# Two k groups instead of one by seven products in each gate/up pair, with one weight sum made by an accumulating DMA

## The chip, the cores and the metric

The kernel runs on one core of one Trainium2 chip. The metric is device time in microseconds (us). Engines: PE (TensorE matmul), DVE (VectorE), ACT (ScalarE), POOL (GpSimd), SP (SyncE, which here only issues DMAs).

## The reference

A two-layer decoder over 256 tokens of width 2048, in float32: a Mamba-2 mixer, a SwiGLU FFN, forgetting attention on shared keys and values, and another SwiGLU FFN. The change touches the large projections, above all the FFN's first one:

```
def swiglu(h, w_gate_up, w_down):
    g, u = jnp.split(h @ w_gate_up, 2, axis=-1)
    return (jax.nn.silu(g) * u) @ w_down
```

`h` is 256 x 2048, gate and up are 5632 columns each, and `w_down` is 5632 x 2048. Two such FFNs are run, one in each layer.

## The kernel before

**Tiles.** A weight matrix comes in units of 512 k rows by 512 columns (1024 KB), each loaded by one DMA on SP's queue into one of three buffers (`wraw`, RAW = 3). A unit holds four k tiles of 128 rows. For near-float32 accuracy each weight tile is split into a high part (`whi`, rounded by ACT, L260) and a low part (`wlo`, the rest, by DVE, L266), and a matmul is done as three: x high by w high, x high by w low, x low by w high (L506 to L508). A plain unit is split in two pieces of two k tiles, and PE does 12 matmuls of 512 columns for each piece. `whi` and `wlo` have four buffers each (SPL = 4), so a split can run up to four pieces ahead of PE.

**Pairs and crossed groups.** Two neighbouring blocks of 512 columns (gate and up of one block in the FFN) make a pair. For some k groups, given in `crossed`, the pair is computed by a seven-product scheme of the Strassen-Winograd kind: the four quarters of the weights (two k halves by two column blocks: b11, b21 in the gate buffer; b12, b22 in the up buffer) and the four quarters of x (two token halves by two k halves) are combined by sums, and seven products of six matmuls each (`cross_step`, L425 to L427) take the place of eight. The products are called d, g, a, c, e, b, f, and ORDER (L206) is their order in time. Sums of x are made once per slot (`sums_of`, `add_sums`); sums of weights are made on DVE in place, in the raw buffers, in `split_cross` (`add`, L384): four of them per group before the change. The products a, c, d, e are kept in four PSUM banks (`mis`) until the pair's last crossed group is done, and are then put together on DVE (`parts`).

**Which groups.** A gate/up pair has four k groups (0 to 3) and before the change crosses group 2 alone, `(2,)`. There are 11 pairs in each of the two FFNs. The other crossed groups are those of the output projection of the Mamba mixer (4 and 6, in two pairs), of the attention (2, two pairs) and of the two down projections (3, 7 and 3, 6, 9, in two pairs each). That makes 22 + 4 + 2 + 4 + 6 = 38 groups.

**Order of the work.** `stream` writes every engine's instructions in order. Units of a pair go in this order: the left units up to a crossed group, then the right units up to it, then the group, and so on. Loads are issued three units ahead: when the last split that reads a unit has been written, the load of the unit three places later follows on SP (`load_to`), and it waits until that split has run. `split_to` writes splits four pieces ahead of PE's step. Other work (evacuation, transposes into the next stage's x, sums of x) is held in queues by `Flow`, which lets it in where its model of the engines' time says that it is ready; before the first product d of a pair, all that is urgent or next in line is written out (`finish_all(False)`, L413).

Of the kernel before, what the change touches and what calls it, by code (L numbers as in the profile page):

```python
# [12 lines left out]
ALU = mybir.AluOpType  # L13
# [16 lines left out]
NFB = DFF // NB  # L30
# [4 lines left out]
KT = 4  # L35

WOUT, DN0, DN1 = (4, 6), (3, 7), (3, 6, 9)

WARM = 9
RAW = 3  # L40
# [8 lines left out]
C_AN, C_F0, C_KV, C_BN, C_F1 = 0, 16, 32, 48, 64  # L49
# [130 lines left out]
class Unit:  # L180


    def __init__(self, blk, kg, src, width, pieces):
        self.blk, self.kg, self.src, self.width, self.pieces = blk, kg, src, width, pieces
        self.raw = None


class Block:
# [8 lines left out]
class Cross:  # L197
# [5 lines left out]

    ORDER = "dgacebf"  # L206

    def __init__(self, left, right, parts):
        self.left, self.right, self.parts, self.ps = left, right, parts, {}
# [10 lines left out]
def kernel(ctx: ExitStack, tc: tile.TileContext, xT_d, x_d, cols_d, rows_d, wdt_d, win_d,  # L220
# [99 lines left out]
    def pair(xs, sources, done, fills, crossed, parts):  # L320


        both = [Block(xs, d, f) for d, f in zip(done, fills)]
        x = Cross(*both, parts)
        order, rights = [], []
        for kg in range(len(xs)):
            us = [Unit(b, kg, src[kg].rearrange("p (k n) -> p k n", n=NB), NB, [[0, 1], [2, 3]])
                  for b, src in zip(both, sources)]
            if kg in crossed:
                order += rights  # L330
                rights = []
                order.append(Group(x, us, xs[kg], kg == crossed[0], kg == crossed[-1]))
            else:
                for b, u in zip(both, us):
                    b.units.append(u)
                order.append(us[0])
                rights.append(us[1])
        blocks.append(order + rights)
# [8 lines left out]
    def load(u, apart=False, before=None):  # L347
        n = sum(len(p) for p in u.pieces)
        u.raw = wraw.tile([P, n, u.width], F32, tag="wraw", name=nm("wraw"))
        for ks in u.pieces if apart else [range(n)]:  # L350
            if before is not None:
                before(ks)
            nc.sync.dma_start(out=u.raw[:, ks[0]:ks[-1] + 1, :], in_=u.src[:, ks[0]:ks[-1] + 1, :])

    def split_piece(u, ks):
        n = len(ks)
# [19 lines left out]

    def split_cross(x, name):

        (g, u) = (v.raw.rearrange("p (j i) n -> p i j n", i=2) for v in x.units)
        b11, b21, b12, b22 = g[:, 0], g[:, 1], u[:, 0], u[:, 1]  # L380

        def add(out, in0, in1):
            flow.work("V", 1.22, flow.at["E"])
            nc.vector.tensor_tensor(out=out, in0=in0, in1=in1, op=ALU.add)  # L384

        src = {"d": b21, "g": b11, "a": b21, "c": b22, "e": b21, "b": b22, "f": b12}[name]
        hi = wspl.tile([P, 2, NB], F32R, tag="whi", name=nm("whi"))
        lo = wspl.tile([P, 2, NB], F32R, tag="wlo", name=nm("wlo"))
        split_hi(hi, src)
        if name == "g":  # L390
            add(b22, b12, b22)
        if name == "c":
            add(b21, b12, b21)
        split_lo(hi, lo, src)
        ready = flow.work("V", 1.22, flow.work("A", 1.05, flow.at["E"]) + LAT)
        if name == "d":
            add(b21, b21, b22)
        if name == "c":
            add(b22, b11, b21)
        return hi, lo, ready  # L400

    def cross_step(group, name, parts):
# [20 lines left out]
        for p in range(2):  # L423
# [1 line left out]
            nc.tensor.matmul(ps, lhsT=xh, rhs=hi[:, p, :], start=group.first and p == 0 and name not in own, stop=False)  # L425
            nc.tensor.matmul(ps, lhsT=xh, rhs=lo[:, p, :], start=False, stop=False)  # L426
            nc.tensor.matmul(ps, lhsT=xl, rhs=hi[:, p, :], start=False, stop=group.last and p == 1 and name not in own)  # L427
        if group.last and name == "e":
            spawn(x.parts(x))
        flow.work("E", STEP)  # L430
        flow.pump()
# [1 line left out]
    def stream(pre_load, pre_split):  # L433
# [12 lines left out]
        def load_to(n):  # L446
            while loaded[0] < min(n, len(units)):
                i = loaded[0]
                if i in pre_load:
                    pre_load[i]()  # L450
                load(units[i], i < 2, load_x0 if i == 0 else None)
                loaded[0] += 1

        def split_to(n):
            for i in range(len(parts), min(n, len(pieces))):
                u, ks = pieces[i]
                if isinstance(u, Group):
                    parts[i] = split_cross(u, ks)
                    if ks in "ef":
                        load_to(units.index(u.units["ef".index(ks)]) + 1 + RAW)  # L460
                    continue
                if i in pre_split:
                    pre_split[i]()
                parts[i] = split_piece(u, ks)
                if ks is u.pieces[-1]:
                    load_to(units.index(u) + 1 + RAW)
# [205 lines left out]
    def ffn_up(xs, r, gu_d, summed):  # L672
# [37 lines left out]
        for nb in range(NFB):  # L710
            x = [None]

            def took(y, x=x):
                x[0] = y
                return parts(y)

            pair(xs, gu_d[2 * nb:2 * nb + 2], (lambda ps, x=x: gate(x[0], ps), lambda ps, x=x, nb=nb: up(x[0], ps, nb)),
                 (None, acts[nb]), (2,), took)
        return acts


# [306 lines left out]
    for g in range(G):  # L1028
        wide(xs1, win_d[12 + g], z_done(g))

    xs2, r2 = out_stage(ys, wout_d, C_F0, WOUT, summed=(2,))
    act0 = ffn_up(xs2, r2, gu0_d, DN0)


# [176 lines left out]
        else:  # L1211
            wide(xsq, wv_d[j], v_done(j), wcol=C_KV)

    xs4, r4 = out_stage(oT, wo_d, C_F1, (2,), summed=(2,))
    act1 = ffn_up(xs4, r4, gu1_d, DN1)
    out_v = out_d.rearrange("(t p) d -> p t d", p=P)

# [103 lines left out]
```

## Time and profile before

| | us |
|---|---|
| median of three runs | 2517.35 (2516.65 to 2519.01) |
| profiled execution, its own time | 2517.21 |
| its span (first to last instruction) | 2515.4 |
| PE busy in the span | 2502.9 |
| DVE busy | 1938.8 |
| ACT busy | 1370.1 |
| DMA queue of SP | 52.5% of 16 engines' span |

Busy time of PE counts overlapping pipelined matmuls as one stretch. A matmul's length in the trace (0.39 us) is longer than the distance from one start to the next; it is the distance that sets the pace. DVE's instructions overlap a little in the same way (a length of 1.22 us, starts 1.14 us apart).

### The profile page before, as it was taken

How to read it: one execution, taken by the hardware profiler on the slowest of the kernel's cores; microseconds unless marked ns; L12 is line 12 of the kernel's file. 1: busy time of each engine (PE TensorE's matmuls, PEld its weight loads, DVE VectorE, ACT ScalarE, POOL GpSimd, SP SyncE). 2: the span in 40 equal slices, each digit the busy share in tenths (PEclk: the TensorE clock that was granted, in tenths of full speed). 3: DMA queues.
4: the chain of work that ended last, by engine and by line, in shares of the span. 5: the costliest groups of instructions: out<-in, count | busy, mean ns of one | idle time of the engine just before them, and what ended most of it. 6: DMA issues, size and time to landing. Idle time of an engine off the chain costs nothing.

```text
span 2515.4 us, 30043 instructions
## 1 busy us (share of the span) xinstructions
PE 2502.9 (100%) x11542; PEld 2076.0 (83%) x11542; DVE 1938.8 (77%) x2499; ACT 1370.1 (54%) x1733; POOL 39.5 (2%) x52
## 2 busy tenths in 40 slices
PE   9999999999999999999999999999999999999999
PEld 7888888887878888888888888888878888888887
DVE  7777777778788878788767667678887878879767
ACT  6665566555555555455545555655555555555544
POOL 0000000000000000000000000000000000000000
PEclk9999999999999999999999999999999999999999
DMA  7655455445554646465565555444555564645564
GB/s 269 223 175 174 178 182 203 167 168 196 186 203 168 218 167 223 178 217 184 181 216 187 200 175 203 163 168 170 182 182 203 184 215 169 219 167 206 200 230 150
DMA packets 68319, 481.11 MB, mean 191 GB/s; under 512 B 7600, under 2 KB 8256, under 8 KB 10576
## 3 DMA queue, kind: packets, MB, share of 16 engines
q1 hardware_dynamic: 66672, 468.64, 52.5%
q0 software_dynamic: 1504, 10.57, 1.0%
q8 instruction: 90, 1.47, 0.2%
q14 instruction: 53, 0.43, 0.0%
HBM read 477.00 MB, written 2.18 MB: 190 GB/s over the span
## 4 chain that ended last, share of the span: by engine, by line
PE 96%; DVE 3%; DMA 1%; ACT 0%; issue 0%; SPq 0%; ACTq 0%; DVEq 0%
PE acc L506 26%; PE acc L507 26%; PE acc L508 26%; PE mis L426 2%; PE mis L427 2%; PE mis L425 2%; PE acc L425 2%; PE acc L427 2%; PE acc L426 2%; PE mis L539 1%; DVE wlo L266 1%; PE mis L967 1%; DVE wraw L384 1%; PE mis L837 0%; DMA xraw<-in_xT_dram 0%; PE mis L973 0%
## 5 line engine op out<-in xcount | busy, mean ns | idle before, releaser
L266 DVE TENSOR_TENSOR wlo<-wraw,whi 128x1024 fp32r<-128x1024 f32 (+1 forms) x899 | 1079.7, 1220 | 349.1 <-ACT whi L260 341.2
L260 ACT CAST whi<-wraw 128x1024 fp32r<-128x1024 f32 (+1 forms) x902 | 929.4, 1049 | 740.4 <-PE acc L508 544.5
L506 PE MATMUL acc<-whi,xT 128*128 128x512 f32 x2816 | 1107.2, 393 | 0.5 <-ACT whi L260 0.4
L507 PE MATMUL acc<-wlo,xT 128*128 128x512 f32 x2816 | 1097.4, 390 | 1.0 <-DVE wlo L266 0.7
L508 PE MATMUL acc<-whi,xT 128*128 128x512 f32 x2816 | 1097.5, 390 | 0.0
L508 PEld LDWEIGHTS acc<-whi,xT 128*128 128x128 f32 x2816 | 528.9, 188 | 110.8
L507 PEld LDWEIGHTS acc<-wlo,xT 128*128 128x128 f32 x2816 | 529.4, 188 | 109.9 <-DVE wlo L266 2.6
L506 PEld LDWEIGHTS acc<-whi,xT 128*128 128x128 f32 x2816 | 529.3, 188 | 109.1 <-issue 1.2
L268 DVE SCALAR_TENSOR_TENSOR wlo<-wraw,cols,whi 128x512 fp32r<-128x512 f32 x192 | 134.6, 748 | 70.8 <-ACT whi L262 70.3
L262 ACT ACTIVATE whi<-wraw,cols 128x512 fp32r<-128x512 f32 x192 | 127.5, 717 | 72.2 <-PE acc L508 67.1
L384 DVE TENSOR_TENSOR wraw<-wraw,wraw 128x1024 f32<-128x1024 f32 x76 | 93.0, 1224 | 3.3 <-DMA wraw<-in_wout_dram 1.0
L384 DVE TENSOR_TENSOR wraw<-wraw 128x1024 f32<-128x1024 f32 x76 | 93.1, 1225 | 2.6
L426 PE MATMUL mis<-wlo,xS 128*128 128x512 f32 x228 | 89.5, 393 | 4.2 <-DVE wlo L266 4.2
L427 PE MATMUL mis<-whi,xS 128*128 128x512 f32 x228 | 88.7, 389 | 0.0
L425 PE MATMUL mis<-whi,xS 128*128 128x512 f32 x228 | 88.7, 389 | 0.0
L266 DVE TENSOR_TENSOR xT<-mis,xT 128x512 fp32r<-128x512 f32 x52 | 33.5, 686 | 37.2 <-ACT xT L260 37.2
L260 ACT CAST xT<-mis 128x512 fp32r<-128x512 f32 x52 | 27.9, 590 | 53.4 <-PE mis L539 53.4
L425 PE MATMUL acc<-whi,xT 128*128 128x512 f32 x144 | 56.1, 389 | 0.0
L427 PE MATMUL acc<-whi,xT 128*128 128x512 f32 x144 | 56.0, 389 | 0.0
L426 PE MATMUL acc<-wlo,xT 128*128 128x512 f32 x144 | 56.0, 389 | 0.0
L426 PEld LDWEIGHTS mis<-wlo,xS 128*128 128x128 f32 x228 | 42.8, 188 | 15.9 <-DVE wlo L266 7.3
L526 POOL TENSOR_TENSOR rs<-ms,mhalf 128x4 f32<-128x4 f32 (+1 forms) x27 | 30.2, 1119 | 1494.8 <-DVE ms L524 1494.5
(241 smaller groups left out, 1890.7 us busy)
## 6 DMA issues: line engine op xcount, KB each, us to landing
wraw<-in_gu_dram SPq DMA_DIRECT2D x176, 1024.0 KB, 4.9
wraw<-in_dn_dram SPq DMA_DIRECT2D x88, 1024.0 KB, 4.9
wraw<-in_win_dram SPq DMA_DIRECT2D x78, 1024.0 KB, 4.9
wraw<-in_wout_dram SPq DMA_DIRECT2D x32, 1024.0 KB, 5.0
wraw<-in_wq_dram SPq DMA_DIRECT2D x16, 1024.0 KB, 5.0
wraw<-in_wk_dram SPq DMA_DIRECT2D x16, 1024.0 KB, 4.9
wraw<-in_wv_dram SPq DMA_DIRECT2D x16, 1024.0 KB, 4.9
wraw<-in_wo_dram SPq DMA_DIRECT2D x16, 1024.0 KB, 4.9
```

What stands on the lines that cost most here:

```text
L260: nc.scalar.copy(out=hi, in_=src)
L262: nc.scalar.activation(hi, src, AF.Copy, scale=scal)
L266: nc.vector.tensor_tensor(out=lo, in0=src, in1=hi.bitcast(F32), op=ALU.subtract)
L268: nc.vector.scalar_tensor_tensor(out=lo, in0=src, scalar=scal, in1=hi.bitcast(F32), op0=ALU.mult, op1=ALU.subtract)
L384: nc.vector.tensor_tensor(out=out, in0=in0, in1=in1, op=ALU.add)
L425: nc.tensor.matmul(ps, lhsT=xh, rhs=hi[:, p, :], start=group.first and p == 0 and name not in own, stop=False)
L426: nc.tensor.matmul(ps, lhsT=xh, rhs=lo[:, p, :], start=False, stop=False)
L427: nc.tensor.matmul(ps, lhsT=xl, rhs=hi[:, p, :], start=False, stop=group.last and p == 1 and name not in own)
L506: nc.tensor.matmul(b.ps[t], lhsT=xh, rhs=hi[:, j, :], start=k == 0, stop=False)
L507: nc.tensor.matmul(b.ps[t], lhsT=xh, rhs=lo[:, j, :], start=False, stop=False)
L508: nc.tensor.matmul(b.ps[t], lhsT=xl, rhs=hi[:, j, :], start=False, stop=k == nk - 1)
L526: nc.gpsimd.tensor_tensor(out=r, in0=ms, in1=mhalf[:, :width], op=ALU.pow)
```

## The change

`ORDER` becomes d, g, c, e, a, b, f, with another choice of weight sums. Of the four sums of weights per group, three stay on DVE (after the splits of d, c and e), and the one that adds b12 to b22 is made by a DMA: when the up unit has landed, POOL issues a second DMA that reads half of the same unit from HBM (512 KB, in rows of 2 KB) and adds it to the other half in the buffer (`accum_op`). That holds for all crossed groups, those in the projections too. All gate/up pairs but the last of each FFN cross groups 1 and 2, one straight behind the other, instead of 2 alone: 20 pairs gain a group, and there are 58 groups in all. For that, slot 1 of x gets its sums too (`summed=(1, 2)`).

```diff
--- before.py
+++ after.py
@@ -182,7 +182,7 @@
 
     def __init__(self, blk, kg, src, width, pieces):
         self.blk, self.kg, self.src, self.width, self.pieces = blk, kg, src, width, pieces
-        self.raw = None
+        self.raw, self.summed = None, False
 
 
 class Block:
@@ -203,7 +203,7 @@
 
 
 
-    ORDER = "dgacebf"
+    ORDER = "dgceabf"
 
     def __init__(self, left, right, parts):
         self.left, self.right, self.parts, self.ps = left, right, parts, {}
@@ -327,6 +327,7 @@
             us = [Unit(b, kg, src[kg].rearrange("p (k n) -> p k n", n=NB), NB, [[0, 1], [2, 3]])
                   for b, src in zip(both, sources)]
             if kg in crossed:
+                us[1].summed = True
                 order += rights
                 rights = []
                 order.append(Group(x, us, xs[kg], kg == crossed[0], kg == crossed[-1]))
@@ -351,6 +352,9 @@
             if before is not None:
                 before(ks)
             nc.sync.dma_start(out=u.raw[:, ks[0]:ks[-1] + 1, :], in_=u.src[:, ks[0]:ks[-1] + 1, :])
+        if u.summed:
+
+            nc.gpsimd.dma_start(out=u.raw[:, 1:KT:2, :], in_=u.src[:, 0:KT:2, :], accum_op=ALU.add)
 
     def split_piece(u, ks):
         n = len(ks)
@@ -376,27 +380,26 @@
 
     def split_cross(x, name):
 
+
         (g, u) = (v.raw.rearrange("p (j i) n -> p i j n", i=2) for v in x.units)
         b11, b21, b12, b22 = g[:, 0], g[:, 1], u[:, 0], u[:, 1]
 
-        def add(out, in0, in1):
+        def add(out, in0, in1, op=ALU.add):
             flow.work("V", 1.22, flow.at["E"])
-            nc.vector.tensor_tensor(out=out, in0=in0, in1=in1, op=ALU.add)
-
-        src = {"d": b21, "g": b11, "a": b21, "c": b22, "e": b21, "b": b22, "f": b12}[name]
+            nc.vector.tensor_tensor(out=out, in0=in0, in1=in1, op=op)
+
+        src = {"d": b21, "g": b11, "a": b22, "c": b22, "e": b21, "b": b21, "f": b12}[name]
         hi = wspl.tile([P, 2, NB], F32R, tag="whi", name=nm("whi"))
         lo = wspl.tile([P, 2, NB], F32R, tag="wlo", name=nm("wlo"))
         split_hi(hi, src)
-        if name == "g":
-            add(b22, b12, b22)
-        if name == "c":
-            add(b21, b12, b21)
         split_lo(hi, lo, src)
         ready = flow.work("V", 1.22, flow.work("A", 1.05, flow.at["E"]) + LAT)
         if name == "d":
             add(b21, b21, b22)
         if name == "c":
-            add(b22, b11, b21)
+            add(b22, b21, b12, ALU.subtract)
+        if name == "e":
+            add(b21, b11, b21)
         return hi, lo, ready
 
     def cross_step(group, name, parts):
@@ -425,7 +428,7 @@
             nc.tensor.matmul(ps, lhsT=xh, rhs=hi[:, p, :], start=group.first and p == 0 and name not in own, stop=False)
             nc.tensor.matmul(ps, lhsT=xh, rhs=lo[:, p, :], start=False, stop=False)
             nc.tensor.matmul(ps, lhsT=xl, rhs=hi[:, p, :], start=False, stop=group.last and p == 1 and name not in own)
-        if group.last and name == "e":
+        if group.last and name == "a":
             spawn(x.parts(x))
         flow.work("E", STEP)
         flow.pump()
@@ -456,8 +459,8 @@
                 u, ks = pieces[i]
                 if isinstance(u, Group):
                     parts[i] = split_cross(u, ks)
-                    if ks in "ef":
-                        load_to(units.index(u.units["ef".index(ks)]) + 1 + RAW)
+                    if ks in "bf":
+                        load_to(units.index(u.units["bf".index(ks)]) + 1 + RAW)
                     continue
                 if i in pre_split:
                     pre_split[i]()
@@ -715,7 +718,7 @@
                 return parts(y)
 
             pair(xs, gu_d[2 * nb:2 * nb + 2], (lambda ps, x=x: gate(x[0], ps), lambda ps, x=x, nb=nb: up(x[0], ps, nb)),
-                 (None, acts[nb]), (2,), took)
+                 (None, acts[nb]), (1, 2) if nb < NFB - 1 else (2,), took)
         return acts
 
 
@@ -1028,7 +1031,7 @@
     for g in range(G):
         wide(xs1, win_d[12 + g], z_done(g))
 
-    xs2, r2 = out_stage(ys, wout_d, C_F0, WOUT, summed=(2,))
+    xs2, r2 = out_stage(ys, wout_d, C_F0, WOUT, summed=(1, 2))
     act0 = ffn_up(xs2, r2, gu0_d, DN0)
 
 
@@ -1211,7 +1214,7 @@
         else:
             wide(xsq, wv_d[j], v_done(j), wcol=C_KV)
 
-    xs4, r4 = out_stage(oT, wo_d, C_F1, (2,), summed=(2,))
+    xs4, r4 = out_stage(oT, wo_d, C_F1, (2,), summed=(1, 2))
     act1 = ffn_up(xs4, r4, gu1_d, DN1)
     out_v = out_d.rearrange("(t p) d -> p t d", p=P)
```

How the instructions stand on DVE, in the crossed group of a gate/up pair in the first FFN, before the change (a line that writes `wlo` is the low part of one product's split, in the order d, g, a, c, e, b, f; `wraw_1293` is the gate buffer, `wraw_1300` the up buffer):

```order
L266 TENSOR_TENSOR wlo_1312_7670<-wraw_1293_7564,whi_1311_7669 128x1024
L384 TENSOR_TENSOR wraw_1293_7564<-wraw_1293_7564,wraw_1300_7604 128x2x512
L384 TENSOR_TENSOR wraw_1300_7604<-wraw_1300_7604 128x2x512
L266 TENSOR_TENSOR wlo_1314_7687<-wraw_1293_7564,whi_1313_7686 128x1024
L266 TENSOR_TENSOR wlo_1316_7704<-wraw_1293_7564,whi_1315_7703 128x1024
L384 TENSOR_TENSOR wraw_1293_7564<-wraw_1300_7604,wraw_1293_7564 128x2x512
L266 TENSOR_TENSOR wlo_1318_7720<-wraw_1300_7604,whi_1317_7719 128x1024
L384 TENSOR_TENSOR wraw_1300_7604<-wraw_1293_7564 128x2x512
L266 TENSOR_TENSOR wlo_1321_7733<-wraw_1293_7564,whi_1320_7732 128x1024
L266 TENSOR_TENSOR wlo_1324_7745<-wraw_1300_7604,whi_1323_7744 128x1024
L266 TENSOR_TENSOR wlo_1327_7756<-wraw_1300_7604,whi_1326_7755 128x1024
```

Four sums (L384) stand among seven splits.

The same place in the changed kernel, from the last two splits of group 1 (b and f) through the whole of group 2 (`wraw_1267` its gate buffer, `wraw_1288` its up buffer):

```order
L266 TENSOR_TENSOR wlo_1287_7424<-wraw_1257_7241,whi_1286_7423 128x1024
L266 TENSOR_TENSOR wlo_1291_7438<-wraw_1262_7275,whi_1290_7437 128x1024
L266 TENSOR_TENSOR wlo_1295_7451<-wraw_1267_7314,whi_1294_7450 128x1024
L389 TENSOR_TENSOR wraw_1267_7314<-wraw_1267_7314,wraw_1288_7427 128x2x512
L266 TENSOR_TENSOR wlo_1298_7463<-wraw_1267_7314,whi_1297_7462 128x1024
L266 TENSOR_TENSOR wlo_1300_7473<-wraw_1288_7427,whi_1299_7472 128x1024
L389 TENSOR_TENSOR wraw_1288_7427<-wraw_1267_7314,wraw_1288_7427 128x2x512
L266 TENSOR_TENSOR wlo_1302_7484<-wraw_1267_7314,whi_1301_7483 128x1024
L389 TENSOR_TENSOR wraw_1267_7314<-wraw_1267_7314 128x2x512
L266 TENSOR_TENSOR wlo_1304_7495<-wraw_1288_7427,whi_1303_7494 128x1024
L266 TENSOR_TENSOR wlo_1306_7505<-wraw_1267_7314,whi_1305_7504 128x1024
L266 TENSOR_TENSOR wlo_1309_7517<-wraw_1288_7427,whi_1308_7516 128x1024
```

There is no plain piece between f of group 1 and d of group 2. The sum behind d (L389) reads the up buffer, into which the DMA has added, and g's split and all that follow stand behind that sum on DVE.

POOL's instructions at the first gate/up pair of the first FFN in the changed kernel (L357 is the accumulating DMA, L529 a small power for the norm's factor):

```order
L357 DMA wraw_912_5561<-in_gu0_dram 128x2x512
L529 TENSOR_TENSOR rs_947_5744<-ms_946_5742,mhalf_104 128x2
L357 DMA wraw_953_5767<-in_gu0_dram 128x2x512
L357 DMA wraw_994_5947<-in_gu0_dram 128x2x512
L357 DMA wraw_1020_6099<-in_gu0_dram 128x2x512
```

Before the change only the L529 row was here. One DMA for each crossed group has come in, and the factor of the norm stands behind the first of this stage.

## Rows read from the trace of the kernel before

**Rows 1.** Page, parts 1, 2 and 4: busy engines, granted clock, chain.

```profile
PE 2502.9 (100%) x11542; PEld 2076.0 (83%) x11542; DVE 1938.8 (77%) x2499; ACT 1370.1 (54%) x1733; POOL 39.5 (2%) x52
...
PEclk9999999999999999999999999999999999999999
...
PE 96%; DVE 3%; DMA 1%; ACT 0%; issue 0%; SPq 0%; ACTq 0%; DVEq 0%
```

**Rows 2.** Windows: one whole gate/up pair of the first FFN (busy us, count).

```profile
core 0: us, PE busy (x) PEld busy (x) DVE busy (x) ACT busy (x) POOL busy (x), PEclk, DMA share, GB/s
...
973.63:1016.70 43.07, 43.07 (x196) 35.75 (x195) 34.96 (x35) 22.29 (x25) 0.00 (x0) 1.00 0.54 195
```

**Rows 3.** Groups by line and form (count, busy us, mean ns): a split, a sum.

```profile
L266 DVE TENSOR_TENSOR wlo<-wraw,whi 128x1024 fp32r<-128x1024 f32 x897 | 1078.4, 1221 | 347.8 <-ACT whi L260 339.9
...
L384 DVE TENSOR_TENSOR wraw<-wraw,wraw 128x1024 f32<-128x1024 f32 x76 | 93.0, 1224 | 3.3 <-DMA wraw<-in_wout_dram 1.0
```

**Rows 4.** Timeline of PE, one crossed group (start us, length us): d, g, e.

```profile
980.81 0.39 PE L425 MATMUL mis<-whi,xT 128*128 128x512 f32 x1
...
982.17 0.39 PE L425 MATMUL acc<-whi,xT 128*128 128x512 f32 x1
...
986.25 0.39 PE L425 MATMUL mis<-whi,xS 128*128 128x512 f32 x1
```

**Rows 5.** Timeline of DVE, the same group.

```profile
973.94 1.23 DVE L266 TENSOR_TENSOR wlo<-wraw,whi 128x1024 fp32r<-128x1024 f32 x1 [1.50 <-ACT whi L260]
975.20 1.22 DVE L384 TENSOR_TENSOR wraw<-wraw,wraw 128x1024 f32<-128x1024 f32 x1
...
983.40 1.23 DVE L384 TENSOR_TENSOR wraw<-wraw 128x1024 f32<-128x1024 f32 x1
984.54 4.77 DVE L266 TENSOR_TENSOR wlo<-wraw,whi 128x1024 fp32r<-128x1024 f32 x4
```

**Rows 6.** Timeline of SP, the load issue in the same group.

```profile
985.79 0.33 SPq L353 DMA_DIRECT2D wraw<-in_gu_dram  x1
```

**Rows 7.** DMA issues: count, KB each, median us from issue to landing.

```profile
wraw<-in_gu_dram SPq DMA_DIRECT2D x176, 1024.0 KB, 4.9
...
e<-acT_d POOLq DMA_DIRECT2D x8, 1024.0 KB, 5.5
...
cub<-cuT_d POOLq DMA_DIRECT2D x2, 1024.0 KB, 6.4
...
wraw<-in_wdt_dram SPq DMA_DIRECT2D x1, 512.0 KB, 3.6
...
acT_d<-acT POOLq DMA_DIRECT2D x1, 64.0 KB, 2.1
```

**Rows 8.** Timeline of PE, crossed group of the first pair.

```profile
720.15 0.48 PE L425 MATMUL mis<-whi,xT 128*128 128x512 f32 x1
...
725.58 0.50 PE L426 MATMUL mis<-wlo,xS 128*128 128x512 f32 x1 [0.85 <-DVE wlo L266]
...
727.97 0.50 PE L426 MATMUL mis<-wlo,xS 128*128 128x512 f32 x1 [0.74 <-DVE wlo L266]
```

**Rows 9.** Timeline of DVE, the same stretch.

```profile
722.82 0.16 DVE L665 TENSOR_REDUCE tot<-ss 128x2 f32<-128x8 f32 x1 [0.29 <-ACT junk L530]
```

**Rows 10.** Windows at the end of the kernel.

```profile
2511.50:2515.70 4.20, 0.22 (x1) 0.00 (x0) 0.69 (x1) 0.00 (x0) 0.00 (x0) 1.00 0.33 125
2515.80:2516.20 0.40, 0.00 (x0) 0.00 (x0) 0.00 (x0) 0.00 (x0) 0.00 (x0) 0.50 0.06 20
```

**Rows 11.** Timeline of PE at the start of the kernel.

```profile
9.01 0.63 PE L506 MATMUL acc<-whi,xT 128*128 128x512 f32 x1
9.44 0.63 PE L507 MATMUL acc<-wlo,xT 128*128 128x512 f32 x1
```

## Prediction

> **What bounds the kernel now.** The page comes first: PE is busy for 2502.9 us of the 2515.4 us span, the chain that ended last is PE for 96%, and the granted clock is full throughout [rows 1]. So work taken from PE is time saved, as long as the others keep up. The next view is a window of one whole gate/up pair, from which the change takes work: 43.07 us, PE busy all of it, DVE 34.96 us [rows 2]. Then the groups by line: a split's low part on DVE is 1.22 us long, and so is a sum of weights [rows 3]. Last, the timelines of one crossed group, PE against DVE, since the question is how far ahead of PE the splits are. PE begins d at 980.81 and g at 982.17: a product of six matmuls takes 1.36 us, a matmul 0.227 us from start to start [rows 4]. DVE's instructions start 1.14 us after one another, or 1.26 us where a sum takes what was just written [rows 5]. DVE ends d's low part at 975.17, 5.6 us before PE wants it, and e's at 984.54 + 1.22 = 985.76, 0.5 us before PE's e at 986.25 [rows 4, 5]. That is what the reader is to see: one crossed group eats about 5 us of DVE's lead. DVE needs 11 instructions (some 13 us) where PE needs 7 x 1.36 = 9.5 us, and the lead grows again only in the plain pieces, where DVE has one split of 1.14 us for 12 matmuls (2.72 us).
>
> **The change, part by part.**
>
> Work taken from PE: 20 more groups, one product of six matmuls fewer in each: 20 x 6 x 0.227 = 27.2 us. All of it is on the path.
>
> Work added to DVE: a pair has three more splits (14 + 8 for 7 + 12) and two more sums (6 for 4). With 1.22 us each that is 34.96 + 5 x 1.22 = 41 us (a little less by starts) against PE's 43.07 - 1.36 = 41.7 us. DVE just fits, with nothing over. The sum fewer in each of the 38 old groups gains nothing: PE doesn't wait for it.
>
> The second group's load. The gate buffer of group 1 is read last by b's split; there are three buffers, so the up unit of group 2 is loaded into it. Call T the end of b's low part. SP issues at once (985.79, behind e's end at 985.76, where e is the last to read the gate buffer [rows 5, 6]). The unit lands 4.9 us later [rows 7], then POOL issues the adding DMA, which lands L later, then DVE makes the sum behind d (1.14 us from start to start) and g's low part (1.22 us). So g's second matmul can go at T + 4.9 + L + 2.4 = T + 7.3 + L. PE without any lead is at b at T, and has b, f, d and one matmul to do: 4.3 us. It then stands still for 3.0 + L. With the lead that the old order leaves at b (0.5 + 0.2 us) and the one sum that DVE is spared (1.14 us), it is 1.2 + L. I take 3.0 + L, since group 1's own sum comes 4.9 + L behind its load and costs lead first, and DVE has no plain piece between to make it good. Behind the waiting sum on DVE stand g's low part and all other splits; behind those PE.
>
> L is not in the trace: no DMA adds there. It moves 512 KB in, but must read the destination as well. From below: a plain load of 512 KB on SP's queue landed in 3.6 us, and 64 KB on POOL's in 2.1. On POOL's queue 1024 KB took 5.5 and 6.4 us [rows 7]. From above: one behind the other, 3.6 + 5.5 = 9.1 us. Nothing can make it less than nothing, since the sum can't begin before the load has landed. I take L = 6.0, between the two 1024 KB rows, because as many bytes are read and the next unit's load runs beside it. The stall is then 9.0 us in each of 20 pairs: 180 us.
>
> What the Trainium skill would make of L, apart from the sum above: the page "DMA: Bandwidth & Descriptors" (section "Anatomy of one DMA — SWDGE (gpsimd) path") fits a POOL DMA as 2.0 us plus bytes by 436 GB/s. For 512 KB that is an estimate of 3.2 us. The page "Collectives: The Full Stack" (section "The bandwidth ceiling: the fold count and why AG ≠ RS ≠ AR") says that an add in the DMA engine costs a second read, which halves the rate; the estimate is then 4.4 us. No run here has an adding DMA; the fit's 4.4 us for 1024 KB stands against 5.5 and 6.4 us in the trace [rows 7].
>
> Once DVE has no lead, each product whose split has a sum before it comes 2.3 to 2.4 us behind the last, where PE needs 1.36. The trace has this case: in the first pair, where DVE is late, PE waits 0.85 and 0.74 us at just such places [rows 8]. I take 0.8 us three times per pair (the two sums of group 2 behind c and e, one of group 1): 20 x 2.4 = 48 us; the bounds are none and 1.0 us four times.
>
> The 38 old groups: their up buffer comes later by L too. u's load is issued behind a plain split; with the full lead of four pieces PE has 0.4 us of a piece, five pieces and d before it wants g, 15.4 us, against 4.9 + 6.0 + 2.4 = 13.3. It fits with 2 us over, and doesn't where half a piece or more of lead is lost. I take 0.4 us each, 15 us; bounds 0 and, at L = 9.1, 3 us each.
>
> The first pair of each FFN: the group begins two units (10.9 us) earlier, and the tasks that make x for slots 2 and 3 must be written before it. They ended on DVE at 722.8 in the old order, 2.7 us behind PE's d at 720.15 [rows 8, 9], so at the most some 13 us each is uncovered; the sums of slot 1 come to that. I take 5 us each, 10 us.
>
> The clock: PE stands idle some 9 us in each pair. At the kernel's end the granted clock was 0.50, the lower level of 1.2 GHz, after 4.2 us in which PE had done nothing but end a matmul [rows 10]; at the start, before the first entry of the clock's record, matmuls stood 0.43 us apart [rows 11] in place of 0.227. A product at 0.43 us costs 1.2 us more. I take one product per pair, 24 us, since DVE's pace hides the rest; bounds 0 and three products, 72 us.
>
> Traffic (58 x 512 KB, 30 MB) and POOL's issues are hidden: SP's queue takes 52.5% of the DMA engines' time (table above), and POOL is busy 39.5 us in all [rows 1].
>
> Sum: -27 + 180 + 48 + 15 + 10 + 24 = +250 us. On the profiled execution's own 2517.2 us that is 2767 us; it lies 0.1 us from the median of 2517.35, so nothing is to be corrected.
>
> **The rivals.**
>
> *The sum lands fast* (L about 3.6, lead 1.8 us at b): the stall is 4.8 to 6.6 us, the rest 2.4 per pair: 20 x 7.2 = 144 to 180, + 5 + 10 + 12 - 27: 2661 to 2697 us. For it: the 512 KB row; against it: that row is alone on its queue and doesn't read what it writes. The Trainium skill's two estimates (the page on DMA and the one on collectives, above) fall here or just above.
>
> *The sum lands slowly* (L = 9.1): the stall is 12.1 us, group 1 waits about 1 us more, the old groups 3 us each: 20 x 15.5 = 310, + 114 + 10 + 30 - 27: about 2955 us. For it: rows of 2 KB, each read, added and written back; against it: the POOL rows of 1024 KB.
>
> *The stall is covered, and the kernel is faster* (other side). Place: g of group 2. If DVE kept the 5.6 us of lead that it has at d, PE would not wait as long as 7.3 + L is under 4.3 + 5.6, so L under 2.6 us. Then only the 27.2 us remain: 2490 us. For it: 64 KB took 2.1 us; against it: 512 KB took 3.6, and the lead is gone by e [rows 4, 5]. If in that case the sums' 2.4 us per pair stayed, it would be 2538 us or, with half of them, 2514, no change.
>
> *The second sum isn't the wait, DVE is*: DVE's 41 us against 41.7 would show as waits for splits all over the pair and a time near 2540.
>
> **How the numbers follow.** My forecast (L from about 4.5 to 7.5) has 0.57, the fast sum 0.20, the slow sum 0.17, DVE alone 0.01, no change 0.02, the covered stall 0.03. The range goes from the fast sum's lower end, 2660, to 2905, the slow one's nearer part; it leaves out the slower half of the slow case, about 0.09, the 0.06 of the last three, and a little of the fast one. Its own range for the forecast is 2690 to 2850: L moves the pairs by 20 us per us, and the old groups by up to 38 more above some 5.5 us. What a measurement can tell is about 0.2%, 5 us. Faster 0.03, same 0.02, slower 0.95.
>
> **What would show it.** In the changed profile: PE's share falls to about 90%; in each of 20 pairs one gap of some 9 us at L429 (the second matmul of g, group 2), released by DVE's `wlo`, and before it DVE idle at L389, released by the DMA into `wraw`; two gaps of under 1 us behind it; the granted clock dips in these stretches; `wraw` DMAs on POOL's queue with 6 us to landing. Landing in under 4 us, or over 8, moves me to the rivals; no gap at L429 and a time under 2540 would refute the step on the second load.

## The result, and the profile after

The changed kernel takes 2880.72 us (median of four runs, 2873.25 to 2888.02) against 2517.43 us (four runs of the kernel before on the same chip): 1.1442 times as long, with a 95% interval of 1.1408 to 1.1476. That is 363 us more; 250 were forecast. 2880.72 lies inside the whole range (2660 to 2905), but 31 us above 2850, the end of the part that the prediction gave its own forecast (L from about 4.5 to 7.5): it lies where the slow sum was expected.

The page of the changed kernel (2876.51 us, span 2874.8), as in [rows 1]: busy engines, granted clock, chain.

```profile
PE 2571.3 (89%) x11422; PEld 2080.1 (72%) x11422; DVE 2028.2 (71%) x2601; ACT 1429.1 (50%) x1805; POOL 101.3 (4%) x110
...
PEclk9999999999899899889999999999889998999999
...
PE 41%; DVE 25%; DMA 23%; issue 6%; ACT 4%; POOLq 0%; ACTq 0%; SPq 0%; POOL 0%; DVEq 0%
```

PE has 120 matmuls fewer than before, and the chain that ended last is no longer PE's: DVE and DMA have nearly half of it. Of the 359 us by which the span is longer, PE stands idle for 291 (303.5 for 12.5) and is busy for 68.4, although 27 us of products are gone. A good half of that is the lower clock: in the stretches where it was granted, PE is busy 117 us for 275 matmuls, which would take 62 us at 0.227 us each. The groups by line (times seen, busy us and mean ns, then the idle time of that engine ahead of them and who ended it) say what PE waits for:

```profile
L389 DVE TENSOR_TENSOR wraw<-wraw,wraw 128x1024 f32<-128x1024 f32 x116 | 142.1, 1225 | 373.6 <-DMA wraw<-in_gu_dram 204.9
L429 PE MATMUL acc<-wlo,xT 128*128 128x512 f32 x224 | 105.0, 469 | 220.4 <-DVE wlo L266 220.4
...
L429 PE MATMUL mis<-wlo,xS 128*128 128x512 f32 x348 | 157.1, 452 | 54.3 <-DVE wlo L266 54.2
```

The sums of two buffers (L389, those behind d and c, each as long as in [rows 3]) had 3.3 us of idle time ahead of them in all before, and have 373.6 now, most of it ended by a DMA into `wraw`. PE waits 220.4 us at L429 into `acc`, all of it at g, whose split stands behind the sum at d. One long gap of the twenty, by the chain of waits from 920 to 940 us (start us, length us, what):

```profile
921.31 1.24 DVE wlo L266
...
922.56 4.79 DMA wraw<-in_gu_dram
...
928.22 5.82 DMA wraw<-in_gu_dram
...
934.12 1.23 DVE wraw L389
935.35 2.28 DVE wlo L266 x2
```

It reads from top to bottom: b's low part of group 1 ends and frees the buffer, the up unit is loaded (4.79 us), POOL issues the adding DMA (5.82), DVE makes the sum and g's low part. From the end of b's split at 922.54 to PE's second matmul of g at 936.54 it is 14.0 us. Timelines of PE: the end of that wait, the four gaps of the next pair's group 1, and the first pairs of both FFNs ([rows 4, 8] are the same places before).

```profile
936.54 0.80 PE L429 MATMUL acc<-wlo,xT 128*128 128x512 f32 x1 [9.46 <-DVE wlo L266]
...
972.10 0.50 PE L429 MATMUL acc<-wlo,xT 128*128 128x512 f32 x1 [1.12 <-DVE wlo L266]
974.43 0.50 PE L429 MATMUL mis<-wlo,xS 128*128 128x512 f32 x1 [0.66 <-DVE wlo L266]
976.83 0.50 PE L429 MATMUL mis<-wlo,xS 128*128 128x512 f32 x1 [0.74 <-DVE wlo L266]
979.22 0.50 PE L429 MATMUL mis<-wlo,xS 128*128 128x512 f32 x1 [0.74 <-DVE wlo L266]
...
738.12 0.80 PE L428 MATMUL mis<-whi,xS 128*128 128x512 f32 x1 [5.39 <-ACT y L562]
...
2014.18 0.79 PE L428 MATMUL mis<-whi,xS 128*128 128x512 f32 x1 [6.57 <-ACT y L562]
```

Windows (us; busy us and count of PE, PEld, DVE, ACT, POOL; granted clock; DMA share; GB/s) from one long gap to the next, and around one of them:

```profile
936.54:994.54 58.00, 45.20 (x188) 35.66 (x188) 40.28 (x41) 24.98 (x27) 2.19 (x2) 0.91 0.51 163
930.48:940.70 10.22, 4.16 (x10) 3.30 (x11) 6.51 (x6) 3.14 (x3) 0.00 (x0) 0.50 0.28 48
```

A pair takes 58.00 us in place of 43.07 [rows 2]: 14.9 us more. The clock is at half (1.2 GHz) for 10.2 us from inside the gap on, where PE had stood idle; in the whole span there are 25 stretches at half clock, 242 us together. DMA issues (count, KB, median us to landing), against [rows 7]:

```profile
wraw<-in_gu_dram SPq DMA_DIRECT2D x176, 1024.0 KB, 5.6
...
wraw<-in_gu_dram POOLq DMA_DIRECT2D x42, 512.0 KB, 5.9
wraw<-in_dn_dram POOLq DMA_DIRECT2D x10, 512.0 KB, 7.0
```

### The profile page after: what moved, and what is told of

The parts are those of the page before. It is cut to its first block, busy times and chain, and to the rows that moved or that the text cites. A ratio compares the mean times of both kernels' runs of the same rounds, so it can differ in the third digit from the quotient of the medians.

```text
span 2874.8 us, 30334 instructions
## 1 busy us (share of the span) xinstructions
PE 2571.3 (89%) x11422; PEld 2080.1 (72%) x11422; DVE 2028.2 (71%) x2601; ACT 1429.1 (50%) x1805; POOL 101.3 (4%) x110
## 3 DMA queue, kind: packets, MB, share of 16 engines
q0 software_dynamic: 17280, 40.98, 7.3%
## 4 chain that ended last, share of the span: by engine, by line
PE 41%; DVE 25%; DMA 23%; issue 6%; ACT 4%; POOLq 0%; ACTq 0%; SPq 0%; POOL 0%; DVEq 0%
DMA wraw<-in_gu_dram 16%; DVE wlo L266 15%; PE acc L510 12%; PE acc L509 12%; PE acc L511 12%; DVE wraw L389 7%; DMA wraw<-in_dn_dram 4%; ACT whi L260 4%; DMA wraw<-in_wout_dram 2%; PE mis L970 1%; DVE xT L266 1%; DMA wraw<-in_wo_dram 1%; PE mis L542 0%; PE acc L429 0%; DVE d L625 0%
## 5 line engine op out<-in xcount | busy, mean ns | idle before, releaser
L260 ACT CAST whi<-wraw 128x1024 fp32r<-128x1024 f32 (+1 forms) x962 | 980.7, 1047 | 1029.7 <-PE acc L511 308.6
L266 DVE TENSOR_TENSOR wlo<-wraw,whi 128x1024 fp32r<-128x1024 f32 (+1 forms) x959 | 1145.5, 1219 | 272.7 <-ACT whi L260 268.1
L509 PE MATMUL acc<-whi,xT 128*128 128x512 f32 x2496 | 983.3, 394 | 5.5 <-ACT whi L260 2.8
L510 PE MATMUL acc<-wlo,xT 128*128 128x512 f32 x2496 | 973.6, 390 | 0.9 <-DVE wlo L266 0.7
L511 PE MATMUL acc<-whi,xT 128*128 128x512 f32 x2496 | 973.4, 390 | 0.0
L509 PEld LDWEIGHTS acc<-whi,xT 128*128 128x128 f32 x2496 | 469.5, 188 | 103.0 <-issue 4.7
L511 PEld LDWEIGHTS acc<-whi,xT 128*128 128x128 f32 x2496 | 469.2, 188 | 97.9
L389 DVE TENSOR_TENSOR wraw<-wraw,wraw 128x1024 f32<-128x1024 f32 x116 | 142.1, 1225 | 373.6 <-DMA wraw<-in_gu_dram 204.9
L429 PE MATMUL acc<-wlo,xT 128*128 128x512 f32 x224 | 105.0, 469 | 220.4 <-DVE wlo L266 220.4
L429 PEld LDWEIGHTS acc<-wlo,xT 128*128 128x128 f32 x224 | 47.3, 211 | 250.5 <-DVE wlo L266 241.5
L429 PE MATMUL mis<-wlo,xS 128*128 128x512 f32 x348 | 157.1, 452 | 54.3 <-DVE wlo L266 54.2
L428 PE MATMUL mis<-whi,xS 128*128 128x512 f32 x348 | 150.3, 432 | 15.7 <-ACT y L562 12.0
L429 PEld LDWEIGHTS mis<-wlo,xS 128*128 128x128 f32 x348 | 73.0, 210 | 106.4 <-DVE wlo L266 92.9
L430 PE MATMUL mis<-whi,xS 128*128 128x512 f32 x348 | 144.9, 416 | 0.0
L428 PEld LDWEIGHTS mis<-whi,xS 128*128 128x128 f32 x348 | 74.0, 213 | 36.5 <-ACT y L562 12.8
L430 PE MATMUL acc<-whi,xT 128*128 128x512 f32 x224 | 98.3, 439 | 0.0
L428 PE MATMUL acc<-whi,xT 128*128 128x512 f32 x224 | 92.8, 414 | 0.0
L357 POOL DMA_DIRECT2D wraw<-in_gu_dram x42 | 45.8, 1090 | 1163.3 <-DMA wraw<-in_gu_dram 599.5
L430 PEld LDWEIGHTS mis<-whi,xS 128*128 128x128 f32 x348 | 72.5, 208 | 13.9
```

What stands on the lines that cost most here:

```text
L260: nc.scalar.copy(out=hi, in_=src)
L266: nc.vector.tensor_tensor(out=lo, in0=src, in1=hi.bitcast(F32), op=ALU.subtract)
L357: nc.gpsimd.dma_start(out=u.raw[:, 1:KT:2, :], in_=u.src[:, 0:KT:2, :], accum_op=ALU.add)
L389: nc.vector.tensor_tensor(out=out, in0=in0, in1=in1, op=op)
L509: nc.tensor.matmul(b.ps[t], lhsT=xh, rhs=hi[:, j, :], start=k == 0, stop=False)
L510: nc.tensor.matmul(b.ps[t], lhsT=xh, rhs=lo[:, j, :], start=False, stop=False)
```

## The experiments

The theory: in a second crossed group the up unit waits for the buffer that group 1 frees, then for its load, then for the adding DMA, and DVE has no lead left to cover that. The rivals: DVE's added work is what binds; the lower clock is; or the new order of the sums. Ten kernels were run, each timed beside the kernel before, which stayed at 2517.3 to 2517.5 us.

### VectorE makes the sum

```diff
-            nc.gpsimd.dma_start(out=u.raw[:, 1:KT:2, :], in_=u.src[:, 0:KT:2, :], accum_op=ALU.add)
...
         split_lo(hi, lo, src)
+        if name == "d":
+            add(b22, b12, b22)
```

> The changed kernel with the adding DMA taken out: b12 + b22 is made by one more sum on DVE (58 sums of 1.14 us). Theory A (the wait is the chain from b's split of group 1 over the freed buffer, the load, the sum and DVE to g of group 2): L of 5.9 us leaves the chain and 1.14 us comes in, so the one long gap falls from 9.5 to about 4.5 us, the clock mostly stays up, and the time is 2600 to 2660 us. Theory B (DVE's own work is the bound, and the gaps are only where it shows): 66 us more on DVE make it as slow as the changed kernel or slower, 2880 to 2945 us.

Measured: 2653.47 us, 1.054 (1.0524 to 1.0556). So 227 of the 363 us go with the DMA, although DVE has more work. The long gap (timeline of PE) is still there, shorter:

```profile
884.48 0.80 PE L428 MATMUL acc<-wlo,xT 128*128 128x512 f32 x1 [3.94 <-DVE wlo L266]
```

From 9.46 to 3.94 us it lost 5.5: the landing of the DMA (5.82) and POOL's steps ahead of it (0.87), less a sum of 1.14 us by starts. What is left is the freed buffer and the load. DVE as the binding engine falls as the main cause.

### A DMA that copies

The same DMA without the addition.

```diff
-            nc.gpsimd.dma_start(out=u.raw[:, 1:KT:2, :], in_=u.src[:, 0:KT:2, :], accum_op=ALU.add)
+            nc.gpsimd.dma_start(out=u.raw[:, 1:KT:2, :], in_=u.src[:, 0:KT:2, :])
```

> The changed kernel with the same DMA on POOL's queue, same bytes and rows, but copying in place of adding (so b22 is replaced by b12 and not summed). It measures what the adding itself costs. If the add needs a second read that costs time, the copy lands in about 4.5 us in place of 5.9, the gap falls by the same 1.4 us and the time to about 2845 us (20 pairs, and some in the groups of the projections). If adding is free, landing stays at 5.9 and the time at 2880 us.

Measured: 2776.68 us, 1.1031 (1.1014 to 1.1047): 104 us less than with the addition, more than expected. DMA issues, and the queue of POOL's DMAs (packets, MB, share of 16 engines), here and then in the changed kernel:

```profile
wraw<-in_gu_dram POOLq DMA_DIRECT2D x42, 512.0 KB, 4.6
...
q0 software_dynamic: 9856, 40.98, 4.1%
```

```profile
q0 software_dynamic: 17280, 40.98, 7.3%
```

The mean landing time over all 58 falls from 6.65 to 4.92 us. 58 x 1.73 = 100 us: each us of landing time costs about a us in a crossed group, the old ones too (by the timelines of PE, 28 us come back in the 18 groups that stand alone, 34 in the 20 first groups and 33 in the 20 second ones). But the run changes more than the addition: the same bytes go in 17280 - 9856 = 58 x 128 fewer packets, 128 of 4 KB for each DMA in place of 256 of 2 KB, and the instruction on POOL takes 0.72 us in place of 1.09. So the run doesn't show how much of the 1.73 us is the addition's own.

### One crossed group per pair, with the adding DMA

```diff
-                 (None, acts[nb]), (1, 2) if nb < NFB - 1 else (2,), took)
+                 (None, acts[nb]), (2,), took)
```

> One part alone: gate/up pairs cross group 2 alone as before (38 groups in all), with the new order of products and the adding DMA. Theory A: without a second group straight behind, the up unit's load is early, the sum is mostly hidden, and only 0.4 to 1 us per group shows: 2530 to 2560 us. Rival D (the adding DMA's latency costs in every group, the second group is not special): 38 groups of the changed kernel's 58 would carry two thirds of the 363 us: above 2700 us.

Measured: 2644.57 us, 1.0504 (1.0488 to 1.052), neither theory's number: the 38 old groups alone cost 127 us, 3.3 each. A pair in the windows, and timelines of POOL, SP, DVE and PE in it:

```profile
882.04:928.09 46.05, 44.04 (x195) 35.50 (x195) 33.46 (x35) 22.05 (x24) 1.09 (x1) 1.00 0.60 194
```

```profile
870.82 1.09 POOL L357 DMA_DIRECT2D wraw<-in_gu_dram  x1 [44.62 <-DMA wraw<-in_gu_dram]
...
871.00 0.33 SPq L354 DMA_DIRECT2D wraw<-in_gu_dram  x1
...
879.62 1.22 DVE L389 TENSOR_TENSOR wraw<-wraw,wraw 128x1024 f32<-128x1024 f32 x1 [5.93 <-DMA wraw<-in_gu_dram]
...
882.04 0.50 PE L429 MATMUL acc<-wlo,xT 128*128 128x512 f32 x1 [0.94 <-DVE wlo L266]
885.57 0.50 PE L429 MATMUL mis<-wlo,xS 128*128 128x512 f32 x1 [0.47 <-DVE wlo L266]
887.96 0.50 PE L429 MATMUL mis<-wlo,xS 128*128 128x512 f32 x1 [0.74 <-DVE wlo L266]
```

SP issues the next unit's load 0.2 us behind the adding DMA, and this one then lands after 8.7 us (median of the 38: 8.3). DVE stands still for 5.9 us, its lead is gone, and PE loses 3 us of the pair at three gaps of under 1 us.

### PE kept at work through the gap

Thirty-six matmuls with zero weights inside d of each second group, so that PE is not idle there.

```diff
+            if name == "d" and p == 1 and group.near:
+                for _ in range(36):
+                    nc.tensor.matmul(ps, lhsT=zero, rhs=hi[:, 1, :], start=False, stop=False)
```

> The changed kernel with 36 useless matmuls of 512 columns more (weights zero, so nothing is added) inside d of each second group, 8.2 us of work in a gap of 9.5 us, in 20 pairs. Theory A with the clock's part: PE is busy through the gap, the granted clock stays at 1.0, the products behind it run at 0.227 us per matmul, and some 3 us per pair come back: 2820 us (2805 to 2845), faster with 720 matmuls more. Rival E (the clock costs nothing, DVE's pace hides it): 2880 us, or a little more.

Measured: 2859.91 us, 1.1362 (1.1343 to 1.1381). The mean granted clock rises from 0.958 to 0.995, but only 21 us come back, 1.0 per pair. In the timeline of PE, group 2 behind the filled stretch:

```profile
869.51 0.50 PE L435 MATMUL acc<-wlo,xT 128*128 128x512 f32 x1 [0.74 <-DVE wlo L266]
873.05 0.50 PE L435 MATMUL mis<-wlo,xS 128*128 128x512 f32 x1 [0.53 <-DVE wlo L266]
875.44 0.50 PE L435 MATMUL mis<-wlo,xS 128*128 128x512 f32 x1 [0.74 <-DVE wlo L266]
```

The changed kernel has only the long gap there, and none behind it: at full clock PE waits for DVE instead. So the lower clock as the main cost falls.

### A fourth buffer for the second group's up unit

```diff
-        u.raw = wraw.tile([P, n, u.width], F32, tag="wraw", name=nm("wraw"))
+        if u.extra:
+            u.raw = slot([P, n, u.width], F32, "wraw")
+        else:
+            u.raw = wraw.tile([P, n, u.width], F32, tag="wraw", name=nm("wraw"))
...
-            while loaded[0] < min(n, len(units)):
+            while loaded[0] < min(n, len(units)) or loaded[0] < len(units) and units[loaded[0]].extra:
```

The second part issues the load into that buffer at once behind the load ahead of it.

> In 18 of the 20 pairs with two crossed groups the second crossed group's up unit is loaded into a spare 8 KB buffer, a fourth one beside the three of wraw, so its load need not wait for b of group 1 to free a buffer; the adding DMA, the products and the order of the instructions stay. Theory A (the long gap is the chain b of group 1, load, adding DMA): those 18 pairs lose the gap of some 9.5 us and about 1 us of slow clock, 18 x 10.5 = 189 us, so 2690 us or less, down to 2580 if the collision of adding DMA and load in group 1 goes with it. Rival B (two crossed groups in a row ask too much of VectorE, or the adding DMA is late wherever the load starts): the gap stays, 2840 to 2885 us.

Measured: 2743.49 us, 1.0896 (1.088 to 1.0912). The 18 long gaps are gone, as theory A has it, but 137 us come back and not 190 or more. A pair takes 50.55 us; timelines of SP, POOL and PE:

```profile
937.54:988.09 50.55, 44.98 (x189) 34.93 (x189) 40.28 (x41) 25.18 (x27) 2.18 (x2) 0.97 0.59 188
```

```profile
974.03 0.80 SPq L358 DMA_DIRECT2D wraw<-in_gu_dram  x2
...
974.85 1.10 POOL L361 DMA_DIRECT2D wraw<-in_gu_dram  x1 [40.00 <-DVE v L629]
984.34 1.09 POOL L361 DMA_DIRECT2D wraw<-in_gu_dram  x1 [8.40 <-DMA wraw<-in_gu_dram]
...
988.09 0.50 PE L433 MATMUL acc<-wlo,xT 128*128 128x512 f32 x1 [3.12 <-DVE wlo L266]
```

So two loads now go out beside group 1's adding DMA: it lands after 10.75 us (at 985.59), and its gap grows from 1.1 to 3.1 us. The second group's DMA, with no load beside it, takes 5.64. The collision, which the expectation counted on losing, got worse.

### The up unit loaded first

```diff
-                    units += u.units
+                    units += u.units[::-1]
...
-                    if ks in "bf":
-                        load_to(units.index(u.units["bf".index(ks)]) + 1 + RAW)
+                    if ks == "f":
+                        load_to(units.index(u.units[0]) + 1 + RAW)
```

> Within each crossed group the up unit, which has the adding DMA, is loaded before the gate unit, and both loads behind a group are let go at f. Theory A (what the second group waits for is load plus adding DMA in a row): the adding DMA now runs beside the gate unit's load, and the second group waits for that load alone (4 to 5 us in place of 9.5) at d rather than at g, so 20 x 5 us and most of the slow clock come back: 2690 to 2770 us, less if the old groups gain by it too. Rival B (the adding DMA beside a load takes 8 us or more, as in the first crossed groups): the gap stays, 2830 to 2890 us.

Measured: 2684.18 us, 1.0682 (1.0649 to 1.0714), a little under theory A's range. A pair takes 48.4 us. The wait is at d, for the gate unit's load (timelines of POOL, SP, ACT and PE):

```profile
880.87 1.09 POOL L357 DMA_DIRECT2D wraw<-in_gu_dram  x1 [9.09 <-DVE xT L266]
...
887.62 0.33 SPq L354 DMA_DIRECT2D wraw<-in_gu_dram  x1
...
892.61 1.04 ACT L260 CAST whi<-wraw 128x1024 fp32r<-128x1024 f32 x1 [5.32 <-DMA wraw<-in_gu_dram]
...
893.71 0.80 PE L428 MATMUL mis<-whi,xT 128*128 128x512 f32 x1 [2.82 <-ACT whi L260]
```

It is not the overlap that the expectation counted on: the second group's adding DMA goes out at 880.87, lands after 5.77 us with no load beside it, and is done a microsecond before the gate unit's load is issued. With the up unit first, its load and its sum fall beside group 1's products, and the second group waits for a load alone.

### GpSimd makes the sum

```diff
-            nc.gpsimd.dma_start(out=u.raw[:, 1:KT:2, :], in_=u.src[:, 0:KT:2, :], accum_op=ALU.add)
+            nc.gpsimd.tensor_tensor(out=u.raw[:, 1:KT:2, :], in0=u.raw[:, 0:KT:2, :], in1=u.raw[:, 1:KT:2, :], op=ALU.add)
```

> The 58 adding DMAs become 58 adds on GpSimd (128x1024 float32 elements each, in place in the same buffer). No row so far shows how long such an add takes there; VectorE's add of the same tile took 1.22 us, and with 1.2 to 3 us for it theory A (the length of the sum behind the load and its collision with other transfers are the cost) gives the time of the kernel with VectorE's sums, 2653 us, more or less: 2600 to 2700 us. Rival B (GpSimd slows VectorE while it adds, or its add takes 6 us and more): 2780 us and more, and VectorE's own instructions show longer means.

Measured: 2685.43 us, 1.0665 (1.0649 to 1.068). Groups by line and timeline of PE:

```profile
L357 POOL TENSOR_TENSOR wraw<-wraw 128x1024 f32<-128x1024 f32 x58 | 143.7, 2478 | 1623.6 <-DMA wraw<-in_gu_dram 647.3 <-DMA wraw<-in_dn_dram 247.1 <-issue 218.4
```

```profile
895.42 0.79 PE L429 MATMUL acc<-wlo,xT 128*128 128x512 f32 x1 [5.41 <-DVE wlo L266]
```

With a sum behind the load of 5.8 (DMA), 2.5 (GpSimd) and 1.1 us (VectorE) the long gap is 9.46, 5.41 and 3.94 us: it follows the sum's length, with 2.8 to 3.7 us more for the buffer, the load and POOL's steps.

### The new order alone

One crossed group per pair, as above, and VectorE makes the sum.

> One crossed group per pair, as before the change, in the changed order of the sums, and the sum of b12 and b22 made by VectorE and not by an adding DMA: the change's new order alone. Theory A (the 127 us by which one crossed group per pair with the adding DMA is slower than before are the adding DMA's): 2505 to 2545 us. Rival B (a good part of them is the new order of the sums and products): 2570 to 2645 us.

Measured: 2518.36 us, 1.0003 (0.9993 to 1.0012). From its page:

```profile
PE 2502.3 (99%) x11542; PEld 2076.1 (82%) x11542; DVE 1934.8 (77%) x2499; ACT 1365.8 (54%) x1733; POOL 39.6 (2%) x52
```

The new order costs nothing, so the 127 us of the kernel with one group and the adding DMA are that DMA's.

### Both taken away

The fourth buffer, and the sum by VectorE or by GpSimd: the two edits above together.

> The spare buffer for the second crossed group's up unit in 18 pairs, and the sum of b12 and b22 by VectorE in place of the adding DMA: both terms of theory A taken away, the wait for a freed buffer and the adding DMA. VectorE then has 41 + 2 x 1.2 = 43.4 us of work in a pair, against 41.7 us on TensorE and 43.07 us for a pair before. Theory A: the pair goes at VectorE's pace, 43.5 to 45 us, with no long gap and no slow clock, so 2517 + 18 x (0.4 to 1.9) + 2 pairs with the old gap at 4.4 = 2530 to 2565 us. Rival B (something else in two crossed groups in a row costs time, as the order of the products or the clock): 2600 us and more.

> The same spare buffer, and the sum of b12 and b22 by GpSimd (2.48 us each beside VectorE's work in the run with GpSimd's sums) in place of the adding DMA. VectorE's work is then 41 us in a pair and some 0.5 us more for its means, which were 20 ns longer with GpSimd at work. Theory A: if VectorE's wait for the sum fits into what it has over, the pair goes below before's 43.07 us and the time to 2495 to 2515 us; if that wait (2.5 us in each crossed group, 5 us a pair, where VectorE has 2 us over) doesn't fit, the pair is 44 to 46.5 us: 2535 to 2585 us, and this is the likelier. Rival B as for the run with VectorE's sums: 2600 us and more.

Measured: 2583.78 us, 1.0263 (1.0248 to 1.0279), with VectorE; 2599.46 us, 1.0326 (1.0309 to 1.0343), with GpSimd. A pair in the windows of the first, and its gaps on PE:

```profile
913.76:958.63 44.87, 42.62 (x189) 34.35 (x189) 42.56 (x43) 25.15 (x27) 0.00 (x0) 1.00 0.51 188
```

```profile
913.76 0.50 PE L432 MATMUL acc<-wlo,xT 128*128 128x512 f32 x1 [0.98 <-DVE wlo L266]
917.29 0.50 PE L432 MATMUL mis<-wlo,xS 128*128 128x512 f32 x1 [0.52 <-DVE wlo L266]
919.69 0.50 PE L432 MATMUL mis<-wlo,xS 128*128 128x512 f32 x1 [0.74 <-DVE wlo L266]
```

The pair came out in theory A's range, at full clock, with DVE busy 42.6 of 44.9 us; the time was 19 us above that range, since the first pairs, the pairs without the buffer and the places around them still have gaps of 1.3 to 4.6 us. With GpSimd the pair takes 45.57 us, and DVE's own instructions are longer (groups by line):

```profile
L266 DVE TENSOR_TENSOR wlo<-wraw,whi 128x1024 fp32r<-128x1024 f32 (+1 forms) x959 | 1174.5, 1249 | 266.8 <-ACT whi L260 261.2
L393 DVE TENSOR_TENSOR wraw<-wraw,wraw 128x1024 f32<-128x1024 f32 x116 | 150.5, 1297 | 28.2 <-POOL wraw L361 21.5
```

These are 1249 and 1297 ns against 1221 and 1224 in [rows 3]. The Trainium skill ("GPSIMD Engine Reference", section "Specifications") says that GpSimd's ports into SBUF are shared with VectorE, with contention for VectorE's instructions with two inputs there; these rows agree, by 2 to 6%.

No version tried beats the kernel before; that with the new order and one group equals it. Both runs leave one question open: with VectorE's sum DVE has a sum more in each group than in the changed kernel, and with GpSimd's it is slowed, so whether DVE would keep up with three sums in each of two groups, if the fourth cost it nothing, was not shown.

## Why the prediction was right, and where its sum was off

The runs divide the 363 us in steps: 227 come with the adding DMA (2880.7 to 2653.5, VectorE's sum), 70 with the second group's wait for a buffer in 18 of the 20 pairs (2653.5 to 2583.8), and 66 are left. With the steps in the other order, the buffer is 137 us and the DMA 160.

The timeline of PE in the changed kernel divides them by place. A crossed group without any wait takes 42 x 0.2266 = 9.5 us; what each takes above that, from its first matmul to the next step behind it, sums as follows. The prediction's terms stand beside it, its 48 us divided as it says, two thirds to the second groups:

| | measured, us | forecast, us |
|---|---|---|
| 20 second groups | 239 (189 the long gaps, 50 behind them) | 180 + 32 + 24 |
| 18 groups that stand alone, and 18 first of two | 57 + 67 | 15 + 16 |
| first pair of each FFN, first group | 23, of which 4.5 were there before | 10 |
| products saved | -27 | -27 |

With the 7 us that such groups lost before taken off, the lines make 352 us; the spans differ by 359. Of the 113 us that the forecast lacked, 93 lie in the second line. That the time still fell into the range owes to the part of it that was kept for the slow sum, which is what the groups of that line met.

**The second group's load** was right. The chain gives 14.0 us from T, where T + 7.3 + L is 13.1 with the measured L of 5.82; POOL's steps ahead of its issue (0.87 us in the chain) were not counted. The twenty gaps, 8.9 to 10.4 us, sum to 189 us; 180 were forecast.

**L = 6.0 us** was right for the second group alone. The prediction took it "because as many bytes are read and the next unit's load runs beside it", and so for all groups. The runs show 5.6 to 6.1 us where no load was issued beside it or in the 4 us before, 8.0 to 9.3 where one was issued within 0.5 us of it, and 8.7 to 11.2 beside two. So a load that starts beside it, one of the two reasons given for 6.0, would have made it 8 or more; for the second group the number came out right by luck, since its DMA meets only the end of a load that went out 4 to 5 us earlier.

**The 38 old groups at "0.4 us each, 15 us"** is the term that was mis-sized. They were costed at L = 6.0, with 2 us to spare. Their adding DMA goes out with the next unit's load and takes 8.3 us (median): 127 us when no pair has two groups in a row. The prediction's own sum with the 8.7 us shown above is 4.9 + 8.7 + 2.4 - 15.4 = 0.6 us, near the first gap's 0.94; the two gaps behind it, 0.47 and 0.74 us, which DVE's spent lead brings, were not counted there at all. 3.3 us each is above even the bound for L = 9.1. The prediction had said that L above some 5.5 us costs the old groups up to 38 us for each us; it was L there that it had wrong, since it took one L for all places. In the changed kernel 18 groups stand alone, and cost 57 us.

**"0.8 us three times per pair"** had the wrong places. Behind the long gap there are no gaps, where two in each pair were named as a sign: PE at half clock is no faster than DVE there, and the products behind the gap take 2.5 us more in each pair without one. Group 1 has four in the pair shown, 1.12 + 0.66 + 0.74 + 0.74 = 3.3 us, and each also loses the 0.16 us between a matmul's length and its pace. Over the 18 first groups that are not in a first pair it is 67 us, 3.7 each, where the prediction had one gap of 0.8 each.

**The first pairs**: the two waits, 5.39 + 6.57 = 12 us, are near the 10 forecast; with what follows in the same group they cost 23 - 4.5 = 18.5 us more than before.

**The clock**, 24 us, agrees with the run that kept PE at work (21 us came back), and for the reason given: DVE's pace hides the rest. That the rest of the 50 us behind the long gaps is the clock's was not shown; where the clock stayed up, waits for DVE stood in its place.

**DVE "just fits"** was wrong in effect. The rival "DVE is the wait" fell as an account of the 363 us, but stands behind the others: with both costs gone, two groups in a row still take 44.87 us a pair, 1.8 over [rows 2]. DVE's average fits, 42.56 of 44.87 us; the 11 instructions per group of that run (10 in the changed kernel) against 7 products do not where no plain piece stands between two groups.

## What to carry to other kernels

Work moved from an engine to a DMA costs that engine's queue the DMA's landing time wherever the engine's next instruction needs the result, less the lead that the engine has there; ask how much lead the consumer has at that very place, and cost the landing with the transfers that will run beside it, not alone. Two groups that each use up lead need something between them that restores it: an average that fits is not enough. Before adding a second one, check which buffer its load waits for.

## What was not expected of the hardware

- An adding DMA of 512 KB on POOL's queue landed in 5.6 us at the least in the changed kernel, the copy in 3.9; the 1.7 us between them hold the addition, twice the packets, and 0.37 us more for the instruction on POOL. The Trainium skill's two estimates cited in the prediction ("Collectives: The Full Stack" and "DMA: Bandwidth & Descriptors"), 4.4 us with and 3.2 without the addition, are both too low here, by 1.2 and 0.7 us.
- Both kinds suffer beside a load of 1024 KB that is issued within 0.5 us of them: the adding DMA took 8.0 to 9.3 us, and the load 5.6 to 6.1 in place of 4.9; the copy took 5.8 to 6.9, and the load 4.8 to 6.0. Beside two loads the adding DMA took up to 11.2 us (the run with the fourth buffer). What makes them slower was not tried.
- A GpSimd addition of 128x1024 float32 took 2.48 us, twice VectorE's 1.22.
